# Two-layer hybrid encoder trunk: priority for the emptying of projection banks, convolution taps issued one at a time, and transposed-key copies in two groups

## The chip, the cores and the metric

The kernel runs on one core of one Trainium2 chip, in a single launch. The core has a tensor engine (PE, with PEld for its weight loads), a vector engine (DVE), a scalar engine (ACT), GpSimd (POOL), a queue of its own for DMA issue (SP) and 16 DMA engines. The metric is the device time of one execution in microseconds; the median over several executions is compared.

## The reference, cut to what matters

There are two layers of width 2048 on 256 tokens. Each normalises its input, projects it with one large matrix, runs four token mixers, gates each mixer's output and projects it back:

```
h = rms_norm(x, norm_g)
proj = h @ w_in                       # 2048 -> 13*512 + 2*128 + 4*2048 columns
ya = a_bg * conv3(a_cg * a_x) * silu(a_z)                    # A: short gated convolution
yb = attention(rope(norm(q)), rope(norm(k)), v) * silu(b_z)  # B: 8 query heads, 2 key heads
yc = rwkv7_bidir(h, c_r, c_k, c_v, ...) * silu(c_z)          # C: one scan per direction, summed
u  = conv31(d_val * sigmoid(d_gate)) + dw_b                  # D: 31 taps, one weight per channel
yd = silu(layer_norm(u)) * silu(d_z)
bp = einsum('bskc,kcd->bskd', stack([ya, yb, yc, yd]), w_branch)
x  = x + sum_k(sigmoid(gates_k + b_gate_k) * bp_k) @ w_out
```

After the second layer one RMS norm follows. Everything is float32.

## The kernel before

**Main stream.** All matrix weights come as one stream of chunks of 128x1024 float32 (`raw`), 306 per layer, in the order in which they are used. ACT copies a chunk, rounded, into `hi`, and DVE subtracts to get `lo` (`fetch`). There are four `raw` buffers, three `hi` and two `lo`. PE multiplies `hi` with the two halves of the operand (512 columns per matmul) and `lo` with the first half (256 columns). Results gather in banks of PSUM: three banks tagged `mg` for tiles of the input and output projections and the gates (`tile_b`, two chunks per tile), one bank tagged `mb` for every tile of the branch projections (`tile_branch`, one chunk for each two columns of tiles), and four banks tagged `sd` for all side work. `whole` empties an `mg` tile in two steps: ACT copies one half into SBUF and DVE adds the other half. `merge` empties the `mb` tile with one instruction of DVE, (z + 1) x psb, where z is the tanh of the gate.

**Side work.** The mixers are Python generators. After each matmul of the main stream `pump` asks a planner, which keeps its own clocks of PE, DVE and ACT from fixed costs, which generators are due, and lets them emit a step; `yield 0.9` means 0.9 us of the planner's time later. `branch_b` is the attention. `rwkv` is the scan: for each of two directions a preamble (low-rank projections, decay, key norms; the low-rank products are the `sd<-part,rounded` matmuls), then 16 steps prepared by `chunks` and `inverses` and a chain of state updates (`bdS`, `bdT`, `bdE`, `bdM` and `bdR` are the small block-diagonal operands of that chain). Within a `rush` block the planner starts instructions of ACT and DVE `BUSY` later than now. `conv_d` makes the 31 taps, one DVE instruction of 128x256 each, for four channel tiles in each layer.

**Order.** The program's order is not yet the engines'. The Tile scheduler sets a fixed order per engine out of dependencies and priorities: what is emitted within `high_priority` goes ahead of what is ready at the same time. Up to now these are the splits into `hi` and `lo`, the rsqrt (two table loads of ACT, `preload_act_table_set`, with a logarithm and an exponential between them) and the `rush` blocks. On the chip each engine works its list strictly from first to last.

Of the kernel before, what the change touches and what calls it, by code (L numbers as in the profile page):

```python
# [12 lines left out]
AF = mybir.ActivationFunctionType  # L13
ALU = mybir.AluOpType
# [4 lines left out]
P = 128  # L19
# [6 lines left out]
CH = 64  # L26
# [138 lines left out]
class Engine:  # L165
# [5 lines left out]
    def __getattr__(self, op):  # L171
        f = getattr(self.real, op)

        def call(out, *args, **kw):
# [6 lines left out]
            elif self.name == "tensor":  # L181
                rhs = kw.get("rhs", args[1])
                n = int(np.prod(out.shape[1:]))
# [7 lines left out]
            else:  # L191
                n = max(int(np.prod(x.shape[1:])) for x in (out,) + args if hasattr(x, "shape"))
                cost = 0.06 + n / 960 + (0.07 if op == "scalar_tensor_tensor" else 0) if self.name == "vector" else 0.1 + n / 1200 + (0.09 if hasattr(kw.get("scale"), "shape") or hasattr(kw.get("bias"), "shape") else 0)
                cost *= k.INFL
# [20 lines left out]
class Kern:  # L215
# [3 lines left out]
    RAW = 8  # L219
    BUSY = 0.7  # L220
    SLACK = 0.4
# [6 lines left out]
    LEAD_B = 1.8  # L228
    LEAD_D = 1.0
    DMA = 2.5  # L230
    SLABS = 9
# [245 lines left out]
    def whole(self, out, ps):  # L477

        nc = self.nc
        nc.scalar.activation(out, ps[:, 1], AF.Copy)  # L480
        nc.vector.tensor_tensor(out, ps[:, 0], out, ALU.add)
        return out
# [246 lines left out]
    def conv_d(self, acc, i, u):  # L729
        nc = self.nc  # L730
# [3 lines left out]
        for j in range(1, 31):  # L734
            nc.vector.scalar_tensor_tensor(a, u[:, j:j + S], w(j), a, ALU.mult, ALU.add)
            if j % 3 == 0:
                yield 0.9
        self.f(u)
# [359 lines left out]
    def chunks(self, n, out, bd, al, vv, kb, gs, rd):  # L1098
# [32 lines left out]
        nc.tensor.transpose(ps4[:, 3], al[:, p, ts], self.ident)  # L1131
        for j, src in enumerate((hi, lo)):
            nc.scalar.activation(ex[hi, j, :, CH:], ps4[src, 0:2, CH:], AF.Copy)
            nc.scalar.activation(ex[lo, j, :, CH:], ps4[src, 0:2, 0:CH], AF.Copy)

        for c, src in enumerate((lo, hi)):
            nc.scalar.activation(ex[hi, 2:4, c, CH:], ps4[src, 2:4, CH:], AF.Copy)
            nc.scalar.activation(ex[lo, 2:4, c, 0:CH], ps4[src, 2:4, 0:CH], AF.Copy)
        out.append((ex, mk, w))
# [110 lines left out]
    def merge(self, l, br, g, acc, mT, gens):  # L1250
# [11 lines left out]
        if first:  # L1262
            acc[g] = self.a([P, 2, S], True)
            nc.vector.scalar_tensor_tensor(acc[g], z, 1.0, psb, ALU.add, ALU.mult)
        else:
            nc.vector.scalar_tensor_tensor(z, z, 1.0, psb, ALU.add, ALU.mult)
            nc.vector.tensor_tensor(acc[g], acc[g], z, ALU.add)
# [202 lines left out]
```

## Time and profile before

| | before |
|---|---|
| median of 3 runs | 1994.88 us (1991.44 to 1995.14) |
| the profiled execution | 1995.8 us, its span 1993.9 us, mean granted clock of PE 0.989 |
| PE busy | 1934.8 us, 97% of the span |
| DVE busy | 1439.8 us, 72% |
| ACT busy | 1268.9 us, 64% |
| weights brought in | 612 chunks of 512 KB, 3.3 us from issue to landing |

Busy shares are averages over very different stages. While the main stream projects, PE has work without a break; the places where it waits are short stretches of the attention and of the scan. The granted clock is 1 at full speed (2.4 GHz) and one half at the lower level (1.2 GHz); a window's PEclk is the mean over the window. Line 204 of the kernel is the helper through which all engine operations go, so groups are told apart by their tiles.

### The profile page before, as it was taken

To read this page: it belongs to the slowest core of one execution; us is meant where nothing else is said; L and a number is where in the kernel's file an instruction comes from. 1 tells how busy PE (TensorE), PEld (TensorE's weight loads), DVE (VectorE), ACT (ScalarE), POOL (GpSimd) and SP (SyncE) were. 2 spreads that over 40 slices of the span, in tenths; PEclk is the share of its full clock that TensorE was granted. 3 is DMA by queue.
4 is the path that set the end of the run, shared out by engine and by line. 5 is a ranking of instruction groups with operands and counts; after the bars stand their busy time and mean duration, and the time that the engine had idled before them with its cause. 6 is when DMAs were issued, how large, how long until landed. Compare 5 with 4: busy or idle time off the path is not lost.

```text
span 1993.9 us, 32440 instructions
## 1 busy us (share of the span) xinstructions
PE 1934.8 (97%) x12194; PEld 1716.7 (86%) x12194; DVE 1439.8 (72%) x2495; ACT 1268.9 (64%) x2293; POOL 71.6 (4%) x117
## 2 busy tenths in 40 slices
PE   8999999899999999999999999998999999999997
PEld 6888788799988898998888887888999989989986
DVE  7867858967787566666677778589787866566655
ACT  6776666567657766554567766766774577565454
POOL 1001010000101000000000010000001100000000
PEclk9999999899999999999999999999999999999998
DMA  7554443344655345566655554533555544456653
GB/s 247 186 181 165 159 156 117 117 165 166 197 181 180 137 150 179 202 206 205 214 186 185 181 169 143 154 114 138 177 171 187 195 143 159 155 184 207 203 190 136
DMA packets 97693, 343.19 MB, mean 172 GB/s; under 512 B 11808, under 2 KB 12192, under 8 KB 97536
## 3 DMA queue, kind: packets, MB, share of 16 engines
q1 hardware_dynamic: 93312, 331.48, 49.1%
q0 software_dynamic: 3648, 8.59, 1.7%
q8 instruction: 96, 1.57, 0.3%
q10 hardware_dynamic: 576, 1.05, 0.1%
q14 instruction: 61, 0.50, 0.1%
HBM read 332.48 MB, written 8.39 MB: 171 GB/s over the span
## 4 chain that ended last, share of the span: by engine, by line
PE 93%; ACT 3%; DVE 2%; DMA 1%; issue 1%; DVEq 0%; SPq 0%; POOL 0%; ACTq 0%; POOLq 0%
PE mg L204 74%; PE sd L204 9%; PE mb L204 9%; DVE arena L204 1%; DVE lo L204 1%; ACT arena L204 1%; ACT bdE L204 1%; DMA raw<-w 1%; ACT hi L204 1%; DMA scratch<-arena 0%; DMA arena<-xT 0%; ACT bdS L204 0%; ACT L178 0%; ACT bdT L204 0%; ACT bdR L204 0%
## 5 line engine op out<-in xcount | busy, mean ns | idle before, releaser
L204 PE MATMUL mg<-slab,hi 128*128 128x512 f32 x4368 | 1113.7, 396 | 17.1 <-DVE slab L204 9.5
L204 DVE TENSOR_TENSOR lo<-raw,hi 128x1024 fp32r<-128x1024 f32 x612 | 746.6, 1221 | 344.1 <-PE mg L204 247.2
L204 PEld LDWEIGHTS mg<-slab,hi 128*128 128x128 f32 x4368 | 789.6, 190 | 160.9 <-DVE slab L204 10.7
L204 ACT ACTIVATE hi<-raw 128x1024 fp32r<-128x1024 f32 x612 | 646.4, 1057 | 440.4 <-PE mg L204 294.7
L204 PE MATMUL mg<-slab,lo 128*128 128x256 f32 x4368 | 618.4, 285 | 1.7 <-DVE lo L204 1.5
L204 PEld LDWEIGHTS mg<-slab,lo 128*128 128x128 f32 x4368 | 585.9, 191 | 37.5 <-DVE lo L204 3.0
L204 DVE TENSOR_TENSOR arena<-arena 128x512 f32<-128x512 f32 (+16 forms) x389 | 166.1, 432 | 35.2 <-ACT arena L204 24.2
L204 DVE SCALAR_TENSOR_TENSOR arena<-arena,par 128x256 f32<-128x256 f32 x346 | 152.2, 479 | 7.8 <-ACT arena L204 6.7
L204 PE MATMUL mb<-slab,hi 128*128 128x256 f32 (+1 forms) x1040 | 156.8, 288 | 1.0 <-DVE slab L204 0.6
L204 PEld LDWEIGHTS mb<-slab,hi 128*128 128x128 f32 x1040 | 141.1, 192 | 5.7 <-DVE slab L204 0.8
L204 DVE TENSOR_TENSOR arena<-mg,arena 128x256 f32<-128x256 f32 x305 | 126.8, 418 | 18.0 <-ACT arena L204 15.3
L204 ACT ACTIVATE arena<-mg 128x256 f32<-128x256 f32 x241 | 89.7, 377 | 67.4 <-PE mg L204 52.3
L204 ACT ACTIVATE arena<-arena 128x256 f32<-128x256 f32 (+4 forms) x195 | 93.5, 497 | 29.5 <-DVE arena L204 26.1
L204 ACT ACTIVATE arena<-arena,b_gate 128x256 f32<-128x256 f32 x128 | 64.0, 503 | 54.9 <-DVE arena L204 54.4
L204 PE MATMUL mb<-slab,lo 128*128 128x256 f32 x528 | 87.2, 286 | 0.0
L178 ACT ACT_TABLE_LOAD x62 | 79.5, 1283 | 8.3 <-PE sd L204 5.0
L204 PEld LDWEIGHTS mb<-slab,lo 128*128 128x128 f32 x528 | 75.1, 192 | 1.6
L204 ACT ACTIVATE bdE<-sd 64x128 f32<-64x128 f32 x256 | 69.7, 272 | 7.5 <-PE sd L204 4.2
L204 DVE SCALAR_TENSOR_TENSOR slab<-arena,slab 128x512 fp32r<-128x512 f32 (+1 forms) x64 | 35.4, 555 | 34.8 <-ACT slab L204 34.7
L204 ACT ACTIVATE arena<-sd 128x64 f32<-128x64 f32 (+4 forms) x122 | 40.0, 332 | 17.3 <-PE sd L204 15.5
L204 DVE SCALAR_TENSOR_TENSOR arena<-arena 128x256 f32<-128x256 f32 (+1 forms) x80 | 37.1, 473 | 17.6 <-ACT arena L204 16.9
L204 PE MATMUL sd<-arena,bdE 128*128 128x128 f32 (+1 forms) x224 | 45.4, 285 | 3.9 <-ACT arena L204 3.3
(96 smaller groups left out, 1062.2 us busy)
## 6 DMA issues: line engine op xcount, KB each, us to landing
raw<-w SPq DMA_DIRECT2D x612, 512.0 KB, 3.3
arena<-xT SPq DMA_DIRECT2D x4, 512.0 KB, 8.3
scratch<-slab POOLq DMA_DIRECT2D x16, 128.0 KB, 2.7
scratch<-arena POOLq DMA_DIRECT2D x8, 256.0 KB, 4.2
arena<-xT SPq DMA_DIRECT2D x8, 256.0 KB, 3.8
x<-arena SPq DMA_DIRECT2D x8, 256.0 KB, 4.8
arena<-x SPq DMA_DIRECT2D x8, 256.0 KB, 3.6
arena<-lorab POOLq DMA_DIRECT2D x16, 96.0 KB, 2.9
```

Of the source, the lines that this page charges most:

```text
L178: return f(out)
L204: return f(out, *args, **kw)
```

## The change

The copy and the addition of `whole`, and the instruction of `merge` that reads the `mb` bank, are emitted at high priority. `BUSY`, the planner's delay for rushed steps, goes from 0.7 to 1.2, and the planner's cost of an ACT instruction on fewer than 128 partitions rises by 0.07. `conv_d` yields after each tap instead of each third one (30 pauses of 1.0 instead of 10 of 0.9). The eight copies in `chunks` that bring transposed keys into the block-diagonal `E` operands go in two groups, by the half of the partitions they are written to, with a pause of 0.6 between.

```diff
--- before.py
+++ after.py
@@ -190,7 +190,7 @@
                 k.due = max(k.due, k.now + 0.2)
             else:
                 n = max(int(np.prod(x.shape[1:])) for x in (out,) + args if hasattr(x, "shape"))
-                cost = 0.06 + n / 960 + (0.07 if op == "scalar_tensor_tensor" else 0) if self.name == "vector" else 0.1 + n / 1200 + (0.09 if hasattr(kw.get("scale"), "shape") or hasattr(kw.get("bias"), "shape") else 0)
+                cost = 0.06 + n / 960 + (0.07 if op == "scalar_tensor_tensor" else 0) if self.name == "vector" else 0.1 + n / 1200 + (0.09 if hasattr(kw.get("scale"), "shape") or hasattr(kw.get("bias"), "shape") else 0) + (0.07 if out.shape[0] < P else 0)
                 cost *= k.INFL
                 if self.name in k.clk:
                     start = max(k.clk[self.name], k.now)
@@ -217,7 +217,7 @@
     FAR = 1
     INFL = 1.05
     RAW = 8
-    BUSY = 0.7
+    BUSY = 1.2
     SLACK = 0.4
     LEAD = 1.7
     TWAIT = 24.0
@@ -227,6 +227,7 @@
     LEAD_A = 2.0
     LEAD_B = 1.8
     LEAD_D = 1.0
+    TAP = 1.0
     DMA = 2.5
     SLABS = 9
     ARENA = (32 + 474 + 32 + 8 - 8 + 16 - 64 + 128 + 16 + 6 - 88 - 16 - 8 - 16 - 32 * FAR - 32 * PARTS - 16) * 32
@@ -477,8 +478,9 @@
     def whole(self, out, ps):
 
         nc = self.nc
-        nc.scalar.activation(out, ps[:, 1], AF.Copy)
-        nc.vector.tensor_tensor(out, ps[:, 0], out, ALU.add)
+        with self.tc.high_priority():
+            nc.scalar.activation(out, ps[:, 1], AF.Copy)
+            nc.vector.tensor_tensor(out, ps[:, 0], out, ALU.add)
         return out
 
 
@@ -733,8 +735,7 @@
         nc.vector.tensor_scalar(a, u[:, 0:S], w(0), self.dwb2[:, i:i + 1], ALU.mult, ALU.add)
         for j in range(1, 31):
             nc.vector.scalar_tensor_tensor(a, u[:, j:j + S], w(j), a, ALU.mult, ALU.add)
-            if j % 3 == 0:
-                yield 0.9
+            yield self.TAP
         self.f(u)
 
     def branch_d(self, acc, convs, dz):
@@ -1129,13 +1130,14 @@
 
         nc.tensor.matmul(ps4[:, 2], vv[:, p, ts], self.cen, start=True, stop=True)
         nc.tensor.transpose(ps4[:, 3], al[:, p, ts], self.ident)
-        for j, src in enumerate((hi, lo)):
-            nc.scalar.activation(ex[hi, j, :, CH:], ps4[src, 0:2, CH:], AF.Copy)
-            nc.scalar.activation(ex[lo, j, :, CH:], ps4[src, 0:2, 0:CH], AF.Copy)
-
-        for c, src in enumerate((lo, hi)):
-            nc.scalar.activation(ex[hi, 2:4, c, CH:], ps4[src, 2:4, CH:], AF.Copy)
-            nc.scalar.activation(ex[lo, 2:4, c, 0:CH], ps4[src, 2:4, 0:CH], AF.Copy)
+        for h, (dst, cols) in enumerate(((lo, slice(0, CH)), (hi, slice(CH, P)))):
+            for j, src in enumerate((hi, lo)):
+                nc.scalar.activation(ex[dst, j, :, CH:], ps4[src, 0:2, cols], AF.Copy)
+
+            for c, src in enumerate((lo, hi)):
+                nc.scalar.activation(ex[dst, 2:4, c, cols], ps4[src, 2:4, cols], AF.Copy)
+            if h == 0:
+                yield 0.6
         out.append((ex, mk, w))
         yield 0
 
@@ -1261,9 +1263,9 @@
         psb = self.tile_branch(self.ys[br])
         if first:
             acc[g] = self.a([P, 2, S], True)
-            nc.vector.scalar_tensor_tensor(acc[g], z, 1.0, psb, ALU.add, ALU.mult)
-        else:
-            nc.vector.scalar_tensor_tensor(z, z, 1.0, psb, ALU.add, ALU.mult)
+        with self.tc.high_priority():
+            nc.vector.scalar_tensor_tensor(acc[g] if first else z, z, 1.0, psb, ALU.add, ALU.mult)
+        if not first:
             nc.vector.tensor_tensor(acc[g], acc[g], z, ALU.add)
         self.f(z)
         if last:
```

No matmul and no instruction of DVE comes or goes by this; what changes is the order on each engine. The rows that follow are of that order. Names carry buffer numbers, which differ between the two programs; what a row does is told by its tiles and shape.

**PE, layer 0, scan of the first direction, a step that ends in the transposes of the state (`bdS3`).** Before, after the last main-stream row, the scan's rows stand one behind the other:

```order
L204 MATMUL mg_526_3943<-slab_20_208,lo_524_3902 128x256 x4
L204 MATMUL sd_479_3570<-arena_69 128x128
L204 MATMUL sd_484_3612<-consts_70,bdS3_103 128x128
L204 MATMUL sd_488_3638<-bdE1_85,bdT0_77 128x128
L204 MATMUL sd_488_3638<-bdE1_85,bdT0_77 128x64
L204 MATMUL sd_493_3690<-arena_69,bdE1_85 128x128
L204 MATMUL sd_494_3695<-arena_69,bdM1_89 128x128
L204 MATMUL sd_494_3695<-arena_69,bdM1_89 128x64
L204 MATMUL sd_493_3690<-arena_69,bdE1_85 128x64
L204 MATMUL sd_495_3699<-bdR0_91,slab_85_679 128x128 x2
L204 MATMUL sd_496_3709<-consts_70,slab_85_679 128x128 x2
```

Now, at the corresponding step:

```order
L204 MATMUL mg_571_4225<-slab_17_205,hi_564_4161 128x512 x4
L204 MATMUL mg_571_4225<-slab_18_206,hi_564_4161 128x512 x4
L204 MATMUL sd_490_3645<-arena_69 128x128
L204 MATMUL mg_557_4125<-slab_19_207,lo_555_4096 128x256 x4
L204 MATMUL mg_557_4125<-slab_20_208,lo_555_4096 128x256 x4
L204 MATMUL mb_567_4192<-slab_177_1312,lo_560_4129 128x256 x4
L204 MATMUL mb_567_4192<-slab_177_1312,hi_559_4128 128x256 x8
L204 MATMUL mb_567_4192<-slab_177_1312,lo_560_4129 128x256 x3
L204 MATMUL sd_495_3677<-consts_70,bdS3_103 128x128
L204 MATMUL sd_499_3701<-bdE1_85,bdT0_77 128x128
L204 MATMUL sd_499_3701<-bdE1_85,bdT0_77 128x64
L204 MATMUL mb_567_4192<-slab_177_1312,lo_560_4129 128x256
```

Main-stream rows (`mg`, `mb`) now stand between the scan's rows; before, 16 rows of the scan (the ten shown and six more) follow each other with no row of the main stream.

**PE, layer 0, start of the second direction's preamble.** The first row of before is the last use of the `mb` bank ahead of the low-rank product `sd_603`:

```order
L204 MATMUL mb_611_4558<-slab_174_1304,hi_606_4503 128x256 x8
L204 MATMUL mb_611_4558<-slab_174_1304,lo_607_4504 128x256 x4
L204 MATMUL mg_615_4594<-slab_17_205,hi_609_4531 128x512 x3
L204 MATMUL mg_615_4594<-slab_18_206,hi_609_4531 128x512 x3
L204 MATMUL sd_603_4480<-part_599_4457,rounded_203 128x512
L204 MATMUL mg_615_4594<-slab_18_206,hi_609_4531 128x512
```

Between the first low-rank product (`sd_559`, 30 rows ahead of it) and `sd_603` stand 28 rows of the main stream in before. Now the first product is `sd_566`; after its second half come two rows of `lo` with 2 matmuls each, two matmuls `sd_601`, and then the rows below, up to the next product `sd_607`:

```order
L204 MATMUL mg_655_4858<-slab_17_205,hi_648_4786 128x512 x4
L204 MATMUL mg_655_4858<-slab_18_206,hi_648_4786 128x512 x4
L204 MATMUL mg_655_4858<-slab_17_205,lo_649_4787 128x256 x4
L204 MATMUL mg_655_4858<-slab_18_206,lo_649_4787 128x256 x4
L204 MATMUL mg_655_4858<-slab_19_207,hi_653_4824 128x512 x4
L204 MATMUL mg_655_4858<-slab_20_208,hi_653_4824 128x512 x4
L204 MATMUL mg_655_4858<-slab_19_207,lo_654_4825 128x256 x4
L204 MATMUL mg_655_4858<-slab_20_208,lo_654_4825 128x256 x4
L204 MATMUL sd_607_4462<-part_602_4433,rounded_203 128x512 x2
L204 MATMUL mb_651_4821<-slab_177_1312,hi_645_4760 128x256 x8
```

Of the main stream 36 matmuls (16 with 512 columns, 20 with 256) are left between the two products, and the next row behind `sd_607` begins a new tile in the single `mb` bank.

**DVE, the same place.** The instruction that empties the `mb` bank reads `mb`. Before, it stands directly behind a split:

```order
L204 TENSOR_TENSOR lo_610_4532<-raw_605_4501,hi_609_4531 128x1024
L204 TENSOR_TENSOR part_599_4457<-arena_69,part_599_4457 128x512
L204 TENSOR_TENSOR arena_69<-mg_604_4500,arena_69 128x256
L204 TENSOR_TENSOR rd_105<-arena_69 128x512
L204 TENSOR_TENSOR lo_614_4562<-raw_608_4529,hi_613_4561 128x1024
L204 SCALAR_TENSOR_TENSOR arena_69<-arena_69,mb_611_4558 128x512
L204 TENSOR_TENSOR arena_69<-arena_69 128x512
L204 TENSOR_TENSOR lo_618_4598<-raw_612_4559,hi_617_4597 128x1024
L204 TENSOR_SCALAR arena_69<-sd_603_4480 128x512
```

Now:

```order
L204 TENSOR_TENSOR lo_658_4862<-raw_652_4822,hi_657_4861 128x1024
L204 SCALAR_TENSOR_TENSOR arena_69<-arena_69,derived0_187 128x256 x2
L204 TENSOR_SCALAR arena_69<-arena_69 128x512
L204 SCALAR_TENSOR_TENSOR arena_69<-consts_70,arena_69 128x256 x2
L204 TENSOR_TENSOR part_602_4433<-arena_69,part_602_4433 128x512
L204 TENSOR_TENSOR rd_105<-arena_69 128x512
L204 TENSOR_SCALAR arena_69<-sd_607_4462 128x512
L204 SCALAR_TENSOR_TENSOR arena_69<-arena_69,par0_71 128x256 x2
L204 SCALAR_TENSOR_TENSOR slab_577_4249<-arena_69 128x512
L204 SCALAR_TENSOR_TENSOR arena_69<-arena_69 128x512
L204 SCALAR_TENSOR_TENSOR slab_575_4247<-arena_69 128x8x64
L204 TENSOR_SCALAR arena_69<-arena_69,derived0_187 128x256 x2
L204 SCALAR_TENSOR_TENSOR arena_69<-arena_69 128x512
L204 SCALAR_TENSOR_TENSOR slab_577_4249<-arena_69,derived0_187 128x256
L204 SCALAR_TENSOR_TENSOR arena_69<-arena_69,mb_629_4655 128x512
```

Before, splits (`lo`) stand at every third row or so, and the row that empties `mb_611` stands ahead of the one that reads the low-rank product `sd_603`. Now the row that empties `mb_629` is the eighth behind the one that reads `sd_607`, and from `lo_658` the next split is 27 rows on. On ACT, not shown, the rows between the first product and the part of the second are: a table load, the logarithm, a table load, a tanh, the exponential, two splits `hi`, four scalings of 256 columns, three of 256 columns from `sd`, and the copy `part_602`; behind it, waiting for the DVE row that reads `sd_607`, are again a table load, a logarithm, a table load and an exponential.

**PE, layer 1, attention.** Before, 8 rows of the main stream (and one single matmul) stand between the two low-rank products of the keys' norm and its broadcast:

```order
L204 MATMUL sd_1626_11900<-part_1622_11865,rounded_203 128x256
L204 MATMUL mg_1635_11978<-slab_1355_9970,lo_1633_11945 128x256
L204 MATMUL mg_1644_12047<-slab_1352_9967,hi_1637_11981 128x512 x4
L204 MATMUL mg_1644_12047<-slab_1353_9968,hi_1637_11981 128x512 x4
L204 MATMUL mg_1644_12047<-slab_1352_9967,lo_1638_11982 128x256 x4
L204 MATMUL mg_1644_12047<-slab_1353_9968,lo_1638_11982 128x256 x4
L204 MATMUL mg_1644_12047<-slab_1354_9969,hi_1641_12012 128x512 x4
L204 MATMUL mg_1644_12047<-slab_1355_9970,hi_1641_12012 128x512 x4
L204 MATMUL mg_1644_12047<-slab_1354_9969,lo_1642_12013 128x256 x4
L204 MATMUL mg_1644_12047<-slab_1355_9970,lo_1642_12013 128x256 x4
L204 MATMUL sd_1639_11995<-part_1634_11951,rounded_203 128x256 x2
```

Now none stands between `sd_1626` and the first half of `sd_1635`:

```order
L204 MATMUL sd_1626_11897<-part_1622_11862,rounded_203 128x256
L204 MATMUL mg_1644_12045<-slab_1354_9969,lo_1643_12020 128x256 x4
L204 MATMUL mg_1644_12045<-slab_1355_9970,lo_1643_12020 128x256 x4
L204 MATMUL sd_1626_11897<-part_1622_11862,rounded_203 128x256
L204 MATMUL sd_1635_11967<-part_1631_11942,rounded_203 128x256
L204 MATMUL mg_1652_12111<-slab_1352_9967,hi_1646_12048 128x512 x4
L204 MATMUL mg_1652_12111<-slab_1353_9968,hi_1646_12048 128x512 x4
L204 MATMUL mg_1652_12111<-slab_1352_9967,lo_1647_12049 128x256 x4
L204 MATMUL mg_1652_12111<-slab_1353_9968,lo_1647_12049 128x256 x4
```

## Rows read from the trace of the kernel before

**Rows 1.** The page: busy time, share and instructions per engine; then the chain's shares.

```profile
PE 1934.8 (97%) x12194; PEld 1716.7 (86%) x12194; DVE 1439.8 (72%) x2495; ACT 1268.9 (64%) x2293; POOL 71.6 (4%) x117
...
PE 93%; ACT 3%; DVE 2%; DMA 1%; issue 1%; DVEq 0%; SPq 0%; POOL 0%; ACTq 0%; POOLq 0%
```

**Rows 2.** Waits of PE, whole span: total us, times, longest.

```profile
PE sd L204 <- ACT bdS L204: 10.7, 8, 2.4
PE mg L204 <- DVE slab L204: 9.5, 1, 9.5
PE mg L204 <- DVE arena L204: 7.0, 4, 3.5
```

**Rows 3.** Windows: length, busy PE, PEld, DVE, ACT, POOL; granted clock; DMA.

```profile
226.00:248.00 22.00, 18.54 (x100) 15.01 (x99) 20.53 (x54) 12.34 (x27) 0.00 (x0) 1.00 0.42 144
284.00:396.00 112.00, 99.03 (x650) 87.47 (x649) 94.24 (x214) 72.62 (x177) 0.00 (x0) 0.93 0.34 118
...
604.00:673.00 69.00, 66.14 (x527) 58.22 (x526) 44.81 (x81) 52.72 (x121) 3.92 (x6) 1.00 0.46 152
1210.00:1226.00 16.00, 12.59 (x46) 9.59 (x45) 13.74 (x32) 5.17 (x9) 0.00 (x0) 0.79 0.33 116
1272.00:1380.00 108.00, 98.31 (x661) 86.82 (x660) 90.65 (x202) 70.78 (x173) 0.00 (x0) 0.95 0.35 123
1611.00:1654.00 43.00, 40.16 (x262) 35.59 (x261) 26.93 (x53) 33.54 (x88) 0.00 (x0) 1.00 0.41 136
```

**Rows 4.** Timeline of PE, layer 1 attention: start, length, then idle and releaser.

```profile
1208.83 1.12 PE L204 MATMUL mg<-slab,lo 128*128 128x256 f32 x8
1209.79 2.00 PE L204 MATMUL mg<-slab,hi 128*128 128x512 f32 x8
1211.62 1.11 PE L204 MATMUL mg<-slab,lo 128*128 128x256 f32 x8
1215.73 0.46 PE L204 MATMUL sd<-part,rounded 128*128 128x256 f32 x1 [3.00 <-ACT part L204]
...
1217.04 3.75 PE L204 MATMUL mg<-slab,hi 128*128 128x512 f32 x8
1220.59 1.91 PE L204 MATMUL mg<-slab,lo 128*128 128x256 f32 x8
1222.30 1.51 PE L204 MATMUL mg<-slab,hi 128*128 128x512 f32 x5
```

**Rows 5.** Waits of PE between 284 and 396 us.

```profile
PE sd L204 <- ACT bdS L204: 5.5, 4, 2.4
PE sd L204 <- DVE arena L204: 2.7, 1, 2.7
```

**Rows 6.** Groups of ACT by form: busy us, mean ns of one, idle before.

```profile
L204 ACT ACTIVATE hi<-raw 128x1024 fp32r<-128x1024 f32 x612 | 646.4, 1057 | 440.4 <-PE mg L204 294.7 <-DMA raw<-w 33.7 <-issue 33.2
...
L178 ACT ACT_TABLE_LOAD x62 | 79.5, 1283 | 8.3 <-PE sd L204 5.0 <-DVE arena L204 1.2 <-PEq L1461 0.7
...
L204 ACT ACTIVATE arena<-arena,par 128x256 f32<-128x256 f32 x88 | 41.9, 509 | 4.0 <-DVE arena L204 2.9 <-DVE slab L204 0.5
L204 ACT ACTIVATE arena<-arena 128x512 f32<-128x512 f32 x62 | 38.7, 624 | 9.0 <-DVE arena L204 8.6
```

**Rows 7.** Groups of DVE by form, columns as before.

```profile
L204 DVE TENSOR_TENSOR lo<-raw,hi 128x1024 fp32r<-128x1024 f32 x612 | 746.6, 1221 | 344.1 <-PE mg L204 247.2 <-PE mb L204 44.2 <-issue 28.4
L204 DVE SCALAR_TENSOR_TENSOR arena<-arena,par 128x256 f32<-128x256 f32 x346 | 152.2, 479 | 7.8 <-ACT arena L204 6.7
...
L204 DVE SCALAR_TENSOR_TENSOR arena<-arena,mb 128x512 f32<-128x512 f32 x64 | 43.5, 680 | 0.2 <-ACT arena L204 0.2
```

**Rows 8.** Timeline of PE, layer 0, low-rank products of the second direction.

```profile
484.32 0.39 PE L204 MATMUL sd<-part,rounded 128*128 128x512 f32 x1
...
496.04 0.39 PE L204 MATMUL sd<-part,rounded 128*128 128x512 f32 x1
...
500.00 0.39 PE L204 MATMUL sd<-part,rounded 128*128 128x512 f32 x1
```

**Rows 9.** Timeline of ACT, a table load and the instruction after it.

```profile
501.45 1.28 ACT L178 ACT_TABLE_LOAD   x1
502.74 0.63 ACT L204 ACTIVATE arena<-arena 128x512 f32<-128x512 f32 x1
```

## The prediction

> **What bounds the kernel now.** I read the page first. PE is busy 97% of the span and makes 93% of the chain that ended last, DVE is busy for 72% and ACT for 64% [rows 1]. So only two things can change the time: stretches in which PE waits, and stretches in which its clock is low because it waited. Then the waits of PE: 10.7 us on ACT's `bdS` copies in the scan's chain, 9.5 us at the start, which no edit touches, and 7.0 us for a free `mg` bank [rows 2]. Then windows around each place where PE is not full [rows 3]. In each I take as lost the length less PE's busy time, plus busy time x (1 - granted clock). The reader should see that the losses sit in six places:
>
> - attention of layer 0 (226 to 248): 22.0 - 18.54 = 3.5 us;
> - first scan of layer 0 (284 to 396): 13.0 + 0.07 x 99.0 = 19.9;
> - second scan of layer 0 (604 to 673): 2.9;
> - attention of layer 1 (1210 to 1226): 3.4 + 0.21 x 12.6 = 6.0;
> - first scan of layer 1 (1272 to 1380): 9.7 + 0.05 x 98.3 = 14.6;
> - second scan of layer 1 (1611 to 1654): 2.8.
>
> Together that is 49.7 us, all that this change could win. The clock's share is visible in one place: after a wait of 3.0 us, 8 matmuls of 512 columns take 3.55 us from start to start of the next group, and 8 of 256 take 1.71 us; ahead of the wait the same groups took 1.83 and 0.96 us [rows 4]. So PE ran at 1.2 GHz instead of 2.4 GHz, and one such wait costs another 1.72 + 0.75 = 2.5 us behind it. The full-speed spacings, 0.229 us and 0.120 us for one matmul, are the ones I use for cover, which is main-stream work that PE can do between two steps of a dependent chain.
>
> **The change part by part.** No matmul and no vector instruction is added, so every edit costs nothing by itself; it only moves work. Where PE is full throughout, moved DVE or ACT work stays behind PE's matmuls and costs nothing. What must be read is what stands between dependent steps at the six places, and whether a new place appears.
>
> *First scans.* Of the 13.0 us that PE idles in layer 0, 5.5 are waits on `bdS` and 2.7 on one DVE result [rows 5]. In the order of before, two groups of 13 and 16 scan rows follow one another without a main-stream row; each row in them waits for an engine and an answer. In the new order almost every step has 3 to 5 us of main stream ahead of it, and one such group is left, of 9 rows. The taps matter here: three taps at 479 ns each [rows 7] used to fall together every 0.9 us of the planner's time, now one each 1.0. DVE was busy 94.2 of 112 us there [rows 3] and its spread-out work presses less on the splits of 1221 ns. The `bdS` waits were one or two per exposed group, so I leave one, 2.4 us as the longest before, with some clock: 4 us lost instead of 19.9, **-15.9**. It can't win over 19.9; if DVE, and not the chain, is what holds PE there, it wins nothing.
>
> In layer 1 two groups of 13 and 15 rows become one of 11 rows, with a second break near it. Adding the rows' durations over the densest stretch of 22 chunks, DVE still has 83.8 us of work against 69.2 us of matmuls (before 90.5 against 74.5 over 23 chunks), hardly less excess. I take 11 us lost instead of 14.6: **-3.6** (between 0 and -10).
>
> *Second scans.* Both are short of cover at their ends in the new order (two and one breaks), and have lost one elsewhere. I add 1 us each, **+2** (between -2 and +4).
>
> *Attention.* In layer 0 the second low-rank product gets 2.5 us less cover, which lengthens a wait of 0.7 us to 3.2; the transposes of the probabilities, which had 6.5 us of cover and no wait, now stand directly behind the scores. Their chain has a reduction, an exponential and a scaling for each score tile; between 0 and 6.5 I take 3.8. Together 7.0 against 3.5: **+3.5**. In layer 1 the two products `sd_1626` and `sd_1635` stand with nothing between them. ACT has two table loads of 1.28, a logarithm, an exponential and a copy of about 0.5 us each to make in between [rows 6], and DVE two steps of 0.48 [rows 7]: 5.0 us. Behind it two sets of transposes and the product with the values follow each other without cover, two copies of 512 columns at 0.62 with a like time of latency each, 2.5 us, and the clock costs what it did, 2.6. So 10.1 and some latency, 10.3, against 6.0: **+4.3** (0 to +8).
>
> *Start of the second direction, layer 0.* Here PE waits for nothing now: between the low-rank products at 484.32 and 496.04 it is full [rows 8]. In the new order 36 matmuls and two of `sd_601` are left: 16 x 0.229 + 20 x 0.120 + 0.4 = 6.5 us. ACT must make in that time two table loads (2.57), the logarithm and the exponential (2 x 0.62), two splits (2 x 1.06), eight operations of 256 columns (8 x 0.51) and the copy `part_602` (0.62): 10.6 us [rows 6]. DVE adds its part, 0.68. So the product starts at 11.3 us, 4.8 after PE ran out. The next row needs the `mb` bank, which a DVE row frees (680 ns [rows 7]) that is eighth behind the one that reads the product. The product ends at 11.7 us and DVE reads it by 12.4. ACT then has again two loads, a logarithm and an exponential, 3.8 us, to 16.2. The nine vector instructions between are five of 256 columns and four of 512, some 5.0 us at 0.48 and 0.68, to 21.2, and the bank is free at 21.9. If all of them wait for the exponential, PE waits 10.2 us; if only the last few do, 2.6 us of work instead of 5.7, it waits 7.1. I take 9.1, nearer to the first, since the first of the nine waits for ACT. With one clock loss of 2.6, as the window in layer 1, the place costs **+16.5** (between 0, if these rows are early in fact, and 25). What is late next is the split `lo_661`, which stands behind all this on DVE, and through it the following `mg` tile. The edits that put `mb`'s emptying at high priority don't help it, since it waits its turn behind rushed rows that have a high priority too. In layer 1 the same product has 14.7 us of main stream ahead of it, and nothing opens.
>
> *Emptying of `mg` banks.* What is to be won is in the 7.0 us, of which the stretches above already hold all four waits.
>
> The sum: -15.9 - 3.6 + 2.0 + 3.5 + 4.3 + 16.5 = +6.8 us. The profiled execution took 1995.8 us, 0.9 above the median of the three runs, 1994.88. From the execution, **2002.6 us**.
>
> The load took 1283 ns on the mean [rows 6], and the instruction after it began 0.01 us after its end [rows 9]; so I have counted 1.28.
> The Trainium skill, ScalarE: Activation LUTs, section What ACT_TABLE_LOAD costs, gives about 1283 ns for the load and about 1380 ns more to drain, 2.66 us for a switch. This trace agrees with the first figure and shows nothing of the second. By that rule the four loads in the new place would cost 5.5 us more, and the sum would be 2008.
>
> **The rivals.**
>
> *The trap does not open* (faster). If ACT and DVE have the preamble's rows done by the time PE comes to `sd_607` and to the `mb` tile, the 16.5 us fall away: 1986.1. For it: ACT is busy 64% [rows 1] and catches up wherever PE waits; many of these rows may not need the first product. Against it: the table load waits for that product by its semaphore, and everything behind it on ACT stands in line. It decides whether PE waits longer than 2 us at `sd_607`.
>
> *Half of it opens* (same). The second wait needs DVE rows that may be done before the exponential. With 4.8 and 2.6 alone, the place costs 7.4: 1993.5, less than can be told.
>
> *The scan's gain does not come* (slower by more). If DVE's load holds PE in the first scans, as its 94.2 of 112 us [rows 3] allows, the 19.5 us there stay lost and the rest is added: 2022. With half of the gain it would be 2012.
>
> *A switch of tables costs more than its row* (slower by more). Were ACT held after each load by as much again as the load takes, 1.28, four loads would make 2007.7. The row after the load speaks against it [rows 9]. By the Trainium skill (ScalarE: Activation LUTs, What ACT_TABLE_LOAD costs) it would be so.
>
> *Nothing changes.* The new order differs at each place shown, so this needs gain and loss to cancel.
>
> **How the numbers follow.** The likeliest, with the trap open and the scan's gain near what I take, gets 0.44, the slower two together 0.10 (0.08 and 0.02), the closed trap 0.27, half of it or a cancelling 0.19. A measurement tells about 0.2%, 4 us, from no change, so up to 1990.9 is faster and from 1998.9 on slower. From the forecast's case, a little falls below 1998.9; so faster 0.28, same 0.19, slower 0.53. The range goes from the closed trap, 1985, to half of the scan's gain with the rest in full, 2013; the forecast's own case lies between 1998 and 2010.
>
> **What would show it.** In the profile after: few `bdS` waits and a granted clock near 1 in the first scan of layer 0; a wait of about 5 us on `part` and one of 7 to 10 us of an `mb` matmul on a DVE result at the start of the second direction; a wait of 4 to 6 us in layer 1's attention. I am wrong if the `mb` wait is absent, or if the windows of the first scans are as empty as now.

## The result and the profile after

| | before | after |
|---|---|---|
| median | 1995.01 us (1991.44 to 1997.17, 4 runs) | 2011.57 us (2009.63 to 2012.47, 4 runs) |
| the profiled execution, its span | 1995.8 us, 1993.9 us | 2012.47 us, 2010.5 us |
| PE busy | 1934.8 us | 1934.5 us |
| PE idle (span less busy) | 59.1 us | 76.0 us |

The change is slower by 0.8%: after / before is 1.0084, with a 95% interval of 1.0071 to 1.0097. The page after answers to [rows 1]:

```profile
PE 1934.5 (96%) x12194; PEld 1715.7 (85%) x12194; DVE 1440.8 (72%) x2495; ACT 1272.3 (63%) x2297; POOL 71.8 (4%) x117
```

PE, DVE and POOL have as many instructions as before, and PE's busy time changed by 0.3 us. ACT has four instructions more, table loads of 1.28 us near 578, 615, 1566 and 1602 us, where PE has no idle time. So the 16.6 us by which the span grew are idle time of PE, and one looks for them window by window. The waits of PE over the whole span (total us, times, longest), which answer to [rows 2]:

```profile
PE mg L204 <- DVE arena L204: 13.5, 6, 5.7
PE sd L204 <- ACT part L204: 12.1, 3, 4.8
PE mb L204 <- DVE arena L204: 10.7, 1, 10.7
PE sd L204 <- ACT arena L204: 10.2, 9, 4.2
PE mg L204 <- DVE slab L204: 9.3, 2, 8.9
PE sd L204 <- ACT bdS L204: 5.5, 6, 2.8
```

The waits on `bdS` have halved, from 10.7 to 5.5. New are one wait of an `mb` matmul of 10.7 us, 12.1 us on `part` (3.7 before), and two of 5.7 among the `mg` waits. Where they sit is seen in windows (columns as in [rows 3]):

```profile
226.00:248.00 22.00, 15.07 (x62) 11.65 (x61) 17.19 (x44) 10.56 (x23) 0.00 (x0) 0.84 0.31 98
284.00:396.00 112.00, 110.75 (x759) 98.55 (x757) 98.98 (x205) 75.70 (x167) 0.00 (x0) 1.00 0.45 147
470.00:506.00 36.00, 20.04 (x109) 17.63 (x109) 27.93 (x50) 26.44 (x53) 1.54 (x2) 0.72 0.23 77
604.00:673.00 69.00, 69.00 (x549) 61.75 (x549) 47.05 (x88) 47.08 (x97) 5.18 (x8) 1.00 0.59 174
780.00:806.00 26.00, 19.07 (x101) 16.20 (x100) 14.08 (x24) 15.02 (x25) 0.00 (x0) 0.87 0.35 112
1214.00:1252.00 38.00, 30.64 (x162) 24.58 (x161) 30.30 (x74) 20.42 (x38) 0.00 (x0) 0.91 0.39 130
1290.00:1402.00 112.00, 106.00 (x671) 95.05 (x670) 99.03 (x214) 74.97 (x184) 0.00 (x0) 0.95 0.40 132
1766.00:1792.00 26.00, 19.07 (x101) 16.17 (x100) 14.19 (x24) 15.02 (x25) 0.00 (x0) 0.87 0.35 113
```

Before, PE was full at the start of the second direction and at the ends of the two second scans:

```profile
470.00:506.00 36.00, 36.00 (x228) 32.63 (x227) 28.41 (x46) 27.11 (x49) 1.54 (x2) 1.00 0.51 164
780.00:806.00 26.00, 26.00 (x152) 22.95 (x151) 17.46 (x27) 14.19 (x23) 0.00 (x0) 1.00 0.53 183
1766.00:1792.00 26.00, 26.00 (x161) 23.39 (x160) 17.32 (x26) 13.61 (x24) 0.00 (x0) 1.00 0.57 189
```

Length less PE's busy time, beside the same place before (the work of layer 1 has moved to later times, so its windows differ; 1200 to 1260 and 1260 to 1402, which hold both, give the same idle times):

| place | idle before | idle after | difference |
|---|---|---|---|
| attention, layer 0 | 3.5 | 6.9 | +3.4 |
| first scan, layer 0 | 13.0 | 1.2 | -11.8 |
| start of the second direction, layer 0 (470 to 506) | 0 | 16.0 | +16.0 |
| second scan, layer 0: its middle, its end (780 to 806) | 2.9, 0 | 0, 6.9 | +4.0 |
| attention, layer 1 | 3.4 | 7.4 | +4.0 |
| first scan, layer 1 | 9.7 | 6.0 | -3.7 |
| second scan, layer 1: its middle, its end (1766 to 1792) | 2.8, 0 | 0, 6.9 | +4.1 |

The differences sum to +16.0 of the 16.9 us of idle time gained. The reader should see one place that outweighs the scan's gain, and two that nobody waited at before, the ends of the second scans. The first of these, PE's timeline at the start of the second direction (start, length, then idle and releaser), which was without a gap in [rows 8]:

```profile
472.16 1.11 PE L204 MATMUL mg<-slab,lo 128*128 128x256 f32 x8
477.87 0.80 PE L204 MATMUL sd<-part,rounded 128*128 128x512 f32 x1 [4.60 <-ACT part L204]
479.34 0.79 PE L204 MATMUL sd<-part,rounded 128*128 128x512 f32 x1 [0.68 <-DVE part L204]
490.82 2.05 PE L204 MATMUL mb<-slab,hi 128*128 128x256 f32 x8 [10.69 <-DVE arena L204]
```

ACT and then DVE in the same stretch:

```profile
481.47 1.28 ACT L178 ACT_TABLE_LOAD   x1
482.76 0.63 ACT L204 ACTIVATE arena<-arena 128x512 f32<-128x512 f32 x1
483.41 1.28 ACT L178 ACT_TABLE_LOAD   x1
484.70 0.63 ACT L204 ACTIVATE arena<-arena 128x512 f32<-128x512 f32 x1
```

```profile
480.17 0.69 DVE L204 TENSOR_SCALAR arena<-sd 128x512 f32<-128x512 f32 x1
485.37 0.88 DVE L204 SCALAR_TENSOR_TENSOR arena<-arena,par 128x256 f32<-128x256 f32 x2 [4.50 <-ACT arena L204]
...
489.99 0.68 DVE L204 SCALAR_TENSOR_TENSOR arena<-arena,mb 128x512 f32<-128x512 f32 x1
```

Read across the three: the low-rank product waits for `part`; DVE reads its answer at 480.17; ACT makes two table loads, a logarithm and an exponential up to 485.33; DVE, which waited 4.50 us for that, has its rows of the preamble to make, and only then, at 489.99, the row that empties the `mb` bank; PE goes on 0.15 us after that row's end. PE waits 10.69 us for that bank.

At the end of the second scan in layer 0 the same kind of wait falls on an `mg` bank, PE first, then ACT, then DVE:

```profile
793.54 0.51 PE L204 MATMUL mg<-slab,lo 128*128 128x256 f32 x3
799.72 3.78 PE L204 MATMUL mg<-slab,hi 128*128 128x512 f32 x8 [5.66 <-DVE arena L204]
```

```profile
793.77 1.28 ACT L178 ACT_TABLE_LOAD   x1
...
795.77 1.28 ACT L178 ACT_TABLE_LOAD   x1
797.06 0.63 ACT L204 ACTIVATE arena<-arena 128x512 f32<-128x512 f32 x1
798.45 0.38 ACT L204 ACTIVATE arena<-mg 128x256 f32<-128x256 f32 x1 [0.76 <-DVE arena L204]
```

```profile
797.72 0.69 DVE L204 TENSOR_TENSOR arena<-arena 128x512 f32<-128x512 f32 x1 [2.35 <-ACT arena L204]
798.45 0.88 DVE L204 SCALAR_TENSOR_TENSOR arena<-arena,par 128x256 f32<-128x256 f32 x2
799.25 0.96 DVE L204 TENSOR_TENSOR arena<-mg,arena 128x256 f32<-128x256 f32 x2
```

ACT's copy is the first row that reads the bank. It stands on ACT behind the slow chain, up to 797.69, and then waits another 0.76 us for a DVE row that reads nothing from the bank. What the two can share is room in the arena, which both write to. That was the hint for the second group of experiments.

### The profile page after: what moved, and what is told of

Read it like the earlier page. It is cut to its first block, busy times and chain, and to the rows that moved or that the text cites. A ratio compares the mean times of both kernels' runs of the same rounds, so it can differ in the third digit from the quotient of the medians.

```text
span 2010.5 us, 32497 instructions
## 1 busy us (share of the span) xinstructions
PE 1934.5 (96%) x12194; PEld 1715.7 (85%) x12194; DVE 1440.8 (72%) x2495; ACT 1272.3 (63%) x2297; POOL 71.8 (4%) x117
## 5 line engine op out<-in xcount | busy, mean ns | idle before, releaser
L204 DVE TENSOR_TENSOR arena<-arena 128x512 f32<-128x512 f32 (+10 forms) x389 | 166.4, 432 | 35.9 <-ACT arena L204 26.8
L204 PE MATMUL mb<-slab,hi 128*128 128x256 f32 (+1 forms) x1040 | 158.8, 290 | 10.7 <-DVE arena L204 10.7
L178 ACT ACT_TABLE_LOAD x62 | 79.5, 1283 | 8.1 <-PE sd L204 4.9
L204 ACT ACTIVATE bdE<-sd 64x128 f32<-64x128 f32 x256 | 62.6, 269 | 8.6 <-PE sd L204 6.3
L204 DVE SCALAR_TENSOR_TENSOR arena<-arena,mb 128x512 f32<-128x512 f32 x64 | 43.7, 683 | 32.1 <-PE mb L204 24.2
```

Of the source, the lines that this page charges most:

```text
L178: return f(out)
L204: return f(out, *args, **kw)
```

## The experiments

The theory at the start was the prediction's: a gain of the first scans, which needs the spread-out taps, and a loss at the start of the second direction, which comes from where the planner put the preamble. Four kernels undo one part of the change each (the planner's two numbers count as one part). All ratios are to the kernel before, on the same chip.

**Without the priorities** (both `high_priority` blocks of the change taken out; the first is shown):

```diff
-        with self.tc.high_priority():
-            nc.scalar.activation(out, ps[:, 1], AF.Copy)
-            nc.vector.tensor_tensor(out, ps[:, 0], out, ALU.add)
+        nc.scalar.activation(out, ps[:, 1], AF.Copy)
+        nc.vector.tensor_tensor(out, ps[:, 0], out, ALU.add)
```

> The changed kernel without the new priorities of the emptying instructions (whole and merge emitted as before). Theory (the order left by the three planner edits makes the loss): between the low-rank products of the second direction the main stream still has only 6.4 us of work, and the group norm at the end of the second scan still stands right ahead of the emptying of the mg banks, so the waits on part and on the mb bank stay and the time stays near 2011 us (2007 to 2015). Rival (the emptying instructions crowd ACT and DVE because they go first): the long mb wait vanishes and the time falls below 1998 us.

2013.14 us (2011.48 to 2013.38), ratio 1.009 [1.0074, 1.0107]. The `mb` wait stays:

```profile
PE mb L204 <- DVE arena L204: 12.1, 1, 12.1
```

The priorities neither cause the slowdown nor cure it.

**Without the planner's numbers:**

```diff
-    BUSY = 1.2
+    BUSY = 0.7
```

and the term of 0.07 taken out.

> The changed kernel with BUSY back at 0.7 and without the cost of 0.07 for ACT instructions on fewer than 128 partitions. Theory: BUSY is what puts main-stream rows between the scan's steps, and it is also what makes the first scan end late. Without it the idle time in the first scans comes back (groups of 13 and more scan rows without a main-stream row: 2 in layer 0, 3 in layer 1; 10 to 14 us each layer), the waits in the attentions go back to 3.5 us each, and neither the mb wait of 10.7 us nor the mg wait of 5.7 us at the ends of the second scans appears: about 1997 us (1993 to 2002). Rival (the trap belongs to the taps, or to the copies, whatever BUSY is): the mb wait stays and the time is 2015 us or more, since the scan's gain is lost too.

2013.36 us (2010.47 to 2016.28), ratio 1.0098 [1.0077, 1.0119]. The theory's number was wrong. The `mb` wait is there without the planner's new numbers; PE's waits in this kernel begin with it:

```profile
PE mb L204 <- DVE arena L204: 11.6, 1, 11.6
```

In exchange the first scan of layer 0 idles 7.7 of its 112 us and not 1.2, and attention is back near its old loss (3.1 and 3.4 us). So the numbers move cover into the first scans and out of attention, and the new wait isn't theirs.

**Without the single taps:**

```diff
-            yield self.TAP
+            if j % 3 == 0:
+                yield 0.9
```

> The changed kernel with the taps three at a time and pauses of 0.9 as before. Theory: the first scan ends earlier relative to the second direction's start, the main stream has 15 us of work between its low-rank products, so the 16 us of waiting there go; the scans keep their cover (no group of 9 or more scan rows stands without main stream in either layer); the attentions stay at 7 us each: about 1989 us (1984 to 1996), unless the end of the second scan, where an mb tile now waits directly for branch C, costs more than the 6.9 us it costs now. Rival (taps crowd DVE in the first scans, spreading them is where the scan's gain came from): the first scan of layer 0 idles 10 us or more again.

1977.21 us (1977.0 to 1977.98), ratio 0.9913 [0.9897, 0.9928], better than its range. Windows of the first scan, the start of the second direction and the end of the second scan, all of layer 0:

```profile
284.00:396.00 112.00, 111.45 (x777) 100.05 (x776) 98.49 (x207) 80.93 (x189) 0.00 (x0) 1.00 0.42 142
440.00:510.00 70.00, 68.79 (x433) 62.14 (x432) 54.41 (x83) 53.70 (x94) 3.44 (x5) 1.00 0.54 174
780.00:806.00 26.00, 24.92 (x148) 21.98 (x148) 16.67 (x27) 18.54 (x29) 0.00 (x0) 1.00 0.51 176
```

No `mb` wait is left, and the first scan idles 0.55 us with three taps at a time. The prediction's reason for the scan's gain is not needed beside the planner's numbers: DVE is as busy there (98.5 us) as in the kernel after (99.0), and PE waits no longer. Attention keeps its losses (6.9 us in the same 22).

**Without the grouped copies** (the eight copies again in one step, as in the diff's removed lines):

```diff
-            if h == 0:
-                yield 0.6
```

> The changed kernel with the eight copies in one step as before. Theory: without the pause of 0.6 in each of 32 chunks the first scan again ends earlier, 17.7 us of main stream stand between the low-rank products, no trap there (-16 to -20 us); three groups of 9 to 11 scan rows without main stream return in layer 0 (+4 to +9); the end of the second scans keeps its mg wait: about 2000 us (1996 to 2005). Rival (each edit does its own part and the trap is BUSY's alone): the mb wait stays at about 10 us and the time is within 4 us of 2011.

1998.74 us (1996.41 to 2003.85), ratio 1.002 [1.001, 1.003]. No `mb` wait over 0.2 us here either, and 0.2 us of idle time in 440 to 510; the end of the second scan keeps its wait (7.5 of 26 us in layer 0):

```profile
440.00:510.00 70.00, 69.80 (x428) 62.84 (x427) 52.93 (x81) 56.79 (x95) 2.81 (x4) 0.98 0.49 161
```

With the planner's new numbers the wait thus needs both the single taps and the grouped copies, neither of which adds work. That speaks for an alignment and not for the price of one edit.

The second question was why the row that empties `mb` stands so late on DVE, whatever its priority. SBUF is handed out by the kernel's own arena, and `merge` asks for its accumulator `acc[g]`, into which this row writes, at the lowest free address. If that room was given back by the preamble shortly before in program order, the row must follow the preamble's last use of it, at any priority.

**Another room for the accumulator.** The one edit: for `acc[g]` the arena prefers room that was not given back within its last 24 allocations and returns.

```diff
-                key = i if keep else (int(self.when[j:e].max()) > self.tick - self.RECENT, e - i - m, -i)
+                key = (int(self.when[j:j + m].max()) > self.tick - keep, i) if keep else (int(self.when[j:e].max()) > self.tick - self.RECENT, e - i - m, -i)
...
-            acc[g] = self.a([P, 2, S], True)
+            acc[g] = self.a([P, 2, S], 24)
```

> The changed kernel in which only the accumulators of merge take another room of the arena: the lowest one that was not given back within the last 24 allocations or returns, instead of the lowest. In the changed kernel the accumulator that the mb bank at the second direction's start is emptied into lies where the scan's preamble has just given room back, so its instruction must follow the preamble's last rows on DVE, at any priority. Theory (this reuse makes the mb wait): the emptying row now stands 28 rows ahead of the row that reads the low-rank product instead of 8 behind it, the waits of 10.7 us on mb and of 4.6 us on part go; a later part of the preamble is short of main stream instead (a wait of 4 to 10 us): 1996 to 2008 us. Rival (the preamble's burst itself delays the bank, whatever memory is used): a wait of about 10 us at an mb row in the same place stays and the time stays within 4 us of 2011.

1995.31 us (1991.18 to 1998.5), ratio 1.0004 [0.9994, 1.0014]: 16 us below the kernel after, by addresses and the order that follows from them. The seventh row that empties an `mb` bank, the one that PE waited 10.69 us for, was DVE's row 736, at 489.99 us; now it is row 705:

```profile
454.05 0.69 DVE L204 SCALAR_TENSOR_TENSOR arena<-arena,mb 128x512 f32<-128x512 f32 x1 [1.77 <-PE mb L204]
```

It waits for the matmuls of its own bank and for nothing else. The windows at the start of the second direction and at the ends of both second scans:

```profile
470.00:506.00 36.00, 27.18 (x151) 23.98 (x150) 29.83 (x52) 28.96 (x55) 0.92 (x2) 0.83 0.42 136
780.00:806.00 26.00, 24.78 (x140) 21.41 (x140) 18.86 (x30) 17.66 (x28) 0.00 (x0) 1.00 0.55 182
1766.00:1792.00 26.00, 24.49 (x143) 21.32 (x141) 18.07 (x30) 17.30 (x29) 0.00 (x0) 1.00 0.54 176
```

The ends idle 1.2 and 1.5 us instead of 6.9 each. At the start 8.8 are left of 16.0: PE now fills the time with the `mb` tile and then waits for the preamble's next product:

```profile
499.15 0.79 PE L204 MATMUL sd<-part,rounded 128*128 128x512 f32 x1 [8.32 <-ACT part L204]
```

So at the start the reuse of room is shown to hold the emptying row back, and the short cover of the preamble is a second, separate cause, worth about half of the place. At the ends the same edit takes the wait away, but the copy that waited there writes a tile of `c_z` (the tanh behind it takes no `b_gate`) and no accumulator. It gets other room only because the accumulators lie elsewhere, and the order around it changes too; that the room was the cause there is likely and not shown. The edit moves idle time in layer 1 as well: its first scan idles 1.6 us in 1260 to 1402 and not 6.0, and a wait of 5.4 us on `part` opens between 1402 and 1480, where PE was full.

**The planner's numbers alone**, in the kernel before (`BUSY = 1.2` and the term of 0.07):

> The kernel before with BUSY at 1.2 and the cost of 0.07 for ACT instructions on fewer than 128 partitions, nothing else. Theory (a scan whose steps are spread ends later, and what is left of it at the merge of branch C must be done without any main stream): in both layers 78 scan rows follow one another at the end of the second scan with no row of the main stream; at the pace of the exposed groups of before (16 rows in 8 to 10 us) this is 40 to 50 us in each layer, so 2075 us (2050 to 2100), although the first scans idle under 4 us. Rival (spreading the scan is what makes the best version fast, the other edits only open traps): below 1985 us.

2083.77 us, a single run. The first scan of layer 0 idles 1.2 us, as in the kernel after, but at the end of each second scan almost nothing covers the scan; in layer 0 PE has four matmuls of the main stream between 789 and 848 us:

```profile
780.00:880.00 100.00, 70.35 (x379) 61.31 (x378) 39.12 (x86) 58.03 (x154) 0.00 (x0) 0.76 0.19 61
1810.00:1905.00 95.00, 66.42 (x334) 57.71 (x333) 34.31 (x78) 53.97 (x148) 0.00 (x0) 0.71 0.17 51
```

Cover is a fixed stock: pushed into the first scan without a pause in the copies, it runs out in the second. That the pause decides it is seen from the numbers together with the grouped copies, below.

**The taps alone**, in the kernel before (`yield self.TAP` after each):

> The kernel before with the taps one at a time, nothing else. Theory (the taps only shift where the preamble of the second direction falls relative to the merges' arena rooms): one mb bank at the second direction's start is emptied by a row that stands ten rows behind the one that reads the low-rank product, with 23 rows of DVE and no split there: a wait of 8 to 12 us of mb on DVE, first scans as before: 2010 us (2004 to 2016). Rival (one tap at a time frees DVE in the scans): the idle time of the first scans falls by 5 us or more and the time is below 1991 us.

1999.33 us (1996.29 to 2002.11), ratio 1.0017 [1.0008, 1.0027], below its range.

```profile
PE mb L204 <- DVE arena L204: 13.0, 1, 13.0
```

```profile
284.00:396.00 112.00, 105.64 (x742) 94.02 (x741) 95.22 (x209) 80.06 (x193) 0.00 (x0) 1.00 0.39 128
```

Both theories were half right. The single taps alone open the `mb` wait, and they also halve the idle time of the first scan of layer 0, from 13.0 to 6.4 us.

**The kernel after without the term of 0.07** (`BUSY` stays 1.2):

```diff
-                cost = 0.06 + n / 960 + (0.07 if op == "scalar_tensor_tensor" else 0) if self.name == "vector" else 0.1 + n / 1200 + (0.09 if hasattr(kw.get("scale"), "shape") or hasattr(kw.get("bias"), "shape") else 0) + (0.07 if out.shape[0] < P else 0)
+                cost = 0.06 + n / 960 + (0.07 if op == "scalar_tensor_tensor" else 0) if self.name == "vector" else 0.1 + n / 1200 + (0.09 if hasattr(kw.get("scale"), "shape") or hasattr(kw.get("bias"), "shape") else 0)
```

> The changed kernel without the cost of 0.07 for ACT instructions on fewer than 128 partitions; BUSY stays at 1.2. Theory (it is this term that moves the attention's steps, not BUSY): the waits of the attentions go back to 2 to 4 us each (-7 us), the first scan of layer 1 has two groups of 13 and 10 rows without main stream again and idles 8 to 11 us, that of layer 0 has one of 14 (4 to 7 us), the mb wait stays (its emptying row still stands ten rows behind): 2010 us (2003 to 2017). Rival (BUSY alone gives the scan's gain): the first scans idle under 4 us each and the time is below 2004 us.

1991.09 us (1990.63 to 1993.54), ratio 0.9984 [0.9974, 0.9993], 19 us under the forecast. As expected attention is back at 3.1 us in layer 0, and the ends of the second scans are full. But the `mb` wait falls in both layers, and the time is still 20 us better than after:

```profile
PE mb L204 <- DVE arena L204: 16.4, 2, 8.3
```

A change of 0.07 us in the planner's cost of a small copy moves the whole alignment.

**The planner's numbers and the grouped copies**, in the kernel before, without taps and priorities:

```diff
-    BUSY = 0.7
+    BUSY = 1.2
```

with the term of 0.07, and the copies as in the change.

> The kernel before with two of the edits, the new numbers of the planner (BUSY at 1.2 and the cost of 0.07) and the copies in two groups with their pause; taps and priorities as before. Theory (the numbers spread the scan, the pause in the copies lets the second scan end before the merge of branch C, priorities do nothing, taps only shift the preamble onto the accumulator's room): 1977 us (1972 to 1982), as the run without the new taps, with under 1 us of waiting in the first scan of layer 0 and no mb wait. Rival (the early emptying of the mg banks is needed once the scan is spread): mg waits on DVE of 4 us or more in the scans and above 1985 us.

1976.21 us (1975.11 to 1976.31), ratio 0.9908 [0.9888, 0.9928]: the lowest median, 0.9% under the kernel before, though its interval overlaps that of the kernel without the single taps.

```profile
284.00:396.00 112.00, 111.35 (x776) 100.22 (x776) 98.25 (x206) 79.41 (x184) 0.00 (x0) 1.00 0.43 145
440.00:510.00 70.00, 69.46 (x439) 62.93 (x438) 55.65 (x84) 54.26 (x97) 3.45 (x5) 1.00 0.53 175
780.00:806.00 26.00, 24.92 (x145) 21.85 (x145) 16.75 (x27) 18.27 (x30) 0.00 (x0) 1.00 0.51 170
```

Neither the long runs of uncovered scan rows of the numbers alone nor the `mb` wait of the single taps is there. Attention still loses 6.9 us in its 22 in layer 0. The span fell by 19.7 us against the kernel before, and only 10.3 of them are idle time; the other 9.4 are busy time of PE, with the same matmuls:

```profile
PE 1925.4 (98%) x12194; PEld 1710.9 (87%) x12194; DVE 1441.4 (73%) x2495; ACT 1260.9 (64%) x2293; POOL 72.5 (4%) x117
```

The mean granted clock is 0.992 here and was 0.989, and in the first scan of layer 0 it is 1.00 and was 0.93. A stretch without waits also gives back what slow matmuls took.

**The room's edit on top of the kernel without single taps** (with the arena's line as above):

```diff
-            acc[g] = self.a([P, 2, S], True)
+            acc[g] = self.a([P, 2, S], 24)
```

> The changed kernel without the new taps and with the other room for merge's accumulators. Theory (the room takes a wait away only where an emptying row is held by it): the waits of 2 us at the end of each second scan go, the rest stays: 1973 us (1968 to 1979). Rival (the room also brings rows forward that crowd the scans, or the end of the second scan with 12 scan rows in a group costs more): 1980 us or more.

1980.0 us (1975.13 to 1981.59), ratio 0.9925 [0.9904, 0.9946]. Its interval overlaps that of the same kernel without the edit, and the expected gain is not to be seen. That fits the reading that another room gives nothing where no emptying row waits for its room.

**The grouped copies alone**, in the kernel before:

> The kernel before with the copies in two groups, nothing else. Theory (without the planner's numbers the scan stays in the same exposed groups): two groups of 12 and 13 scan rows in layer 0, of 13 and 15 in layer 1, one more of 13 in the second scan; idle time of the first scans within 4 us of 13.0 and 9.7, no mb wait: 1996 us (1990 to 2002). Rival (the pause relieves ACT in the scans by itself): the first scans idle 5 us less each and the time is below 1988 us.

1993.93 us (1993.36 to 1996.11), ratio 1.0001 [0.9991, 1.001]. The first scan of layer 0 idles 8.1 us instead of 13.0, and 600 to 700 idles 7.1: moved, not won.

## Why the prediction was right or wrong

The forecast was 2002.6 us and the measured median is 2011.57, inside the range of 1985 to 2013 and near its upper end. The direction came from the right place, the start of the second direction; the size fell short, most of all in the second scans.

- *What bounds the kernel* held: PE's busy time changed by 0.3 us and the rest is in its idle time. Of the forecast's +6.8, idle time makes about +9.5 (the scan -10.6, the new place +13.9, the others as they stand), against +16.9 measured. The clock makes -2.7 (the scan -5.3, the new place +2.6), against -0.3 in PE's busy time, in which slow matmuls show. I counted the scan's return to full speed (0.93 to 1.00) and the new place's slow stretch (0.72), but not those that open elsewhere: attention in layer 0 goes from 1.00 to 0.84, each end of a second scan from 1.00 to 0.87.
- *First scan, layer 0*: one short group was to be left. Idle time fell from 13.0 to 1.2 us and the `bdS` waits there to 0.2. Right in kind and size, but "the taps matter here" was wrong beside the planner's numbers: without the single taps 0.55 us are idle. Alone they do halve it.
- *First scan, layer 1*: -3.6 forecast, -3.7 in idle time.
- *Attention*: +3.5 and +4.3 forecast, +3.4 and +4.0 in idle time. The wait on `part` in layer 1, which I put at 5.0, is 4.82 us. It is the term of 0.07 that moves the cover away.
- *Start of the second direction*: 4.8 and 9.1 us of waiting forecast, 4.60 and 0.68 and 10.69 found. The upper reading, that all nine DVE rows wait for the exponential, was the true one. The explanation beside it was wrong: the emptying row was not in a queue behind rushed rows of a like priority, for it comes as late without any priority (12.1 us); with another room for the accumulator it goes 31 rows earlier. "In layer 1 nothing opens" held for this change, and in the kernel without the term of 0.07 it did open there, 8.1 us.
- *Second scans*, with *Emptying of `mg` banks*, is the step that fell short: I gave the two scans +2 together, a figure worked out from no row, and under the banks I counted only the four waits of before and no new one. The scans cost +8.1. Both lose their old 2.9 and 2.8 us, but at each end PE idles 6.9 us, 5.66 of them in one wait for an `mg` bank behind a slow chain (two table loads with their function on ACT, then DVE); with another room for the accumulators, and the order that came with it, these ends idle 1.2 and 1.5. I had looked at cover for PE and not at what a row must wait for before it may write. That is 6.1 of the 7.4 us between 9.5 and 16.9; the new place adds 2.1, and the first scan of layer 0 gives 1.2 back.
- *The rivals*: the trap's not opening is what the kernel without the single taps shows, 1977 where I put 1986.1. Half of the scan's gain would have made 2012, which is the time measured, but by chance: the gain of layer 0 came in full. For the same reason it is partly luck that the time lies inside a range whose upper end stood for that case. The dearer switch of tables is refuted once more: after both loads shown above the next row begins 0.01 us later. The Trainium skill (ScalarE: Activation LUTs, What ACT_TABLE_LOAD costs) gives 1283 ns for the load, which 1.28 agrees with, and about 1380 ns more to drain, of which these rows show nothing.

What stays open is which numbers make the preamble and the merges fall together. With single taps the `mb` wait was there at a `BUSY` of 0.7, with the copies in one step or grouped, and at 1.2 with grouped copies; at 1.2 with the copies in one step it was not. No rule was found that tells it ahead, short of the order itself. Which DVE row holds the room was not traced; that it is the room is known for the `mb` wait of the kernel after, from the one edit of addresses. For the `mb` waits of the other kernels, and for the `mg` waits at the ends of the second scans, it is inferred.

## What to carry to other kernels

Where memory is handed out by the kernel's own allocator, a priority can't move a row ahead of the last use of the room that it writes to (here 2013 us without the priorities, 1995 with other room): look for a releaser that has nothing to do with the waiting tile, and try another room before another priority. Edits to a planner do not add up (alone: +88 for the numbers, +4 for the taps, nothing for the copies; the numbers with the copies: -17 to -18), so parts of such a change are to be measured in pairs and by leaving each out. Count idle time and the clock apart and in every place: a change of the span is the change of PE's idle time plus that of its busy time, which holds the slow matmuls (10.3 and 9.4 us in the kernel with the lowest median).
